# Cross-covariance attention on one core: Q and K of four units loaded in rows of 8 KB, in another order of all work

## The chip, the cores and the metric

The kernel runs on one core of a Trainium2 chip. The metric is the device time of one execution in microseconds (us), as a median of runs; lower is better. Engines are named as in the profile: PE (TensorE), DVE (VectorE), ACT (ScalarE), POOL (GpSimd), SP (SyncE, which here only issues transfers).

## The reference

Batch 8, heads 12, sequence 512, head size 64, all in float32. Attention runs over the channels of a head, not over its rows:

```python
Q_norm = Q / (np.linalg.norm(Q, axis=-2, keepdims=True) + 1e-10)
K_norm = K / (np.linalg.norm(K, axis=-2, keepdims=True) + 1e-10)
attn = np.einsum('bhnd,bhne->bhde', Q_norm, K_norm)
attn = np.exp(attn - np.max(attn, axis=-1, keepdims=True))
attn = attn / (np.sum(attn, axis=-1, keepdims=True) + 1e-10)
return np.einsum('bhnd,bhde->bhne', V, attn).astype(np.float32)
```

Q, K, V and the output have 12.6 MB each, so 37.7 MB are read and 12.6 MB written.

## The kernel before

**Units.** The 96 heads are cut into S = 12 units of eight heads, and two units make a pair `w` (W = 6). One load brings 1 MB: Q of a unit, K of a unit, or half of a pair's V. On 128 partitions a unit of Q has four heads with 32 partitions each and 16 rows of the sequence in each partition, twice (`r` = 0, 1), once for either four heads; so a partition gets two runs of 16 x 64 floats, 4 KB each (`Qf`, `Kf`). V (`Vu`) lies with 16 partitions to a head and 32 rows in each, one run of 8 KB. Unit 0 comes in halves (`FINE`), and its loads are issued ahead of everything else, K's by ACT.

**Steps of a unit `s`.**
- `cast_qk` (keys `q0` for Q, `ck` for K): float32 to bf16, by DVE, ACT or POOL.
- `square` (`sq`, `sk`): squares of the bf16 tiles, by ACT or DVE. `sums` (`s1`) adds them over the rows on PE with the mask `hm`; `fold` (`rd`, DVE), `norms` (`nn`, PE) and `powers` (`pw`, ACT: logarithm and exponent) turn the sums into reciprocal norms.
- `grams` (`gr`): 64 matmuls, K transposed times Q, for two heads at a time (128 x 128, of which the two diagonal 64 x 64 blocks count).
- `scale_k` (`kx`, DVE), `logits` (`lg`: four transpositions on PE), `scales_q` (`qs`, two on DVE), `exps` (`ex`, ACT), `normalise` (`nm`, DVE) give the attention matrix `ab` in bf16.
- V of a pair: `cast_v` (`cv`), `vtrans` (`vt`, transposition on PE), `vcopy` (`vc`).
- `outs` (`ou`, PE) and `ocopy` (`oc`, ACT or DVE) make the output tile `so`, and `store` (`st`) writes it: 1 MB for a unit, in halves for units 10 and 11 (`HALF`), in four cuts for unit 9 (`SPLIT`, `CUTS`).

**Buffers.** Seven tiles of 1 MB for Q and K (`qk`), three for V (`v`), two each of the bf16 tiles of Q and K (`qm`) and of the squares (`sq`), six for output (`so`). `gram` holds four banks of PSUM, one tile in all.

**What sets the order.** The schedule is written out before the program is built. `piece` gives each step a key, a cost on each engine that may do it, the steps that it waits for (`after`), those that it only follows (`behind`), and a rank. `Order.run` plays the schedule with these costs: it takes the steps that could begin soonest, within 0.05 us, and of them the one of lowest rank; `BIAS` moves a choice between engines. The result fixes the order of instructions on every engine, SP's issues among them. Ranks come from `R`; those of loads and stores come from paces: a load of Q or K of unit `s` has `QK_PACE * s / 12`, one of V has `V_FROM + V_PACE * w / 6` (half a pair counts one half), a store `V_FROM + V_PACE * (s / 2) / 6 + ST_LAG`. SP works its list in order: a load that waits for a buffer keeps all later issues back. At most eight transfers are under way.

Of the kernel before, what the change touches and what calls it, by code (L numbers as in the profile page):

```python
# [18 lines left out]
 'R': {'ck': 14.3601,  # L19
       'q': -46.9145,  # L20
       'sq': -4.5261,
       'sk': 21.309,
       'gr': 31.9137,
       's1': -8.269,
       'rd': 14.1273,
       'nn': -13.565,
       'pw': -22.1669,
       'kx': 16.8281,
       'lg': -36.3133,
       'qs': 14.727,  # L30
       'ex': 7.4539,
       'nm': 23.5766,
       'cv': -5.1919,
       'vt': 13.5707,
       'vc': 31.4911,
       'ou': -17.6156,
       'oc': 6.4318},
 'BIAS': {('cv', 'DVE'): 12.3272,
          ('vc', 'ACT'): 5.2627,
          ('oc', 'DVE'): 7.9654,  # L40
          ('q0', 'ACT'): -9.0842,
          ('sk', 'ACT'): 4.174,
          ('sk', 'DVE'): 5.4091,
          ('cv', 'ACT'): 0.906,
          ('cv', 'POOL'): -0.1651,
          ('ck', 'DVE'): -11.8527,
          ('ck', 'ACT'): -10.4645,
          ('ck', 'POOL'): -15.4937,
          ('oc', 'ACT'): 4.7795,
          ('sq', 'DVE'): -12.3114,  # L50
          ('sq', 'ACT'): -21.9953,
          ('q0', 'DVE'): -28.6804,
          ('q0', 'POOL'): -29.3142,
          ('vc', 'DVE'): -20.4676},
 'QK_PACE': 0.9356,
 'V_FROM': 0.0874,
 'V_PACE': 0.7666,
 'ST_LAG': 6.0835,
 'SPLIT': 3,
 'HALF': (10, 11),  # L60
 'WAKE': ('SP',),
 'CUTS': ((0, 0, 6, 0, 124), (0, 0, 6, 124, 128), (0, 6, 16, 0, 128), (1, 0, 16, 0, 128))}
# [89 lines left out]
def kernel(  # L152
# [27 lines left out]
    qmp = ctx.enter_context(tc.tile_pool(name="qmp", bufs=NB["qm"]))  # L180
    sqp = ctx.enter_context(tc.tile_pool(name="sqp", bufs=NB["sq"]))
    vtp = ctx.enter_context(tc.tile_pool(name="vtp", bufs=NB["vt"]))
    sop = ctx.enter_context(tc.tile_pool(name="sop", bufs=NB["so"]))
    abp = ctx.enter_context(tc.tile_pool(name="abp", bufs=NB["ab"]))
# [28 lines left out]
    def load_qk(s, x, c):  # L213
        w, e = divmod(s, 2)
        if (s, x) not in qk32:
            qk32[s, x] = qp.tile([128, T, D], F32, name="qk32")
        issue = nc.scalar if (s, x) == (0, 1) and PAR["ACTQ"] else nc.sync
        o = qk32[s, x][:, cols(c)].rearrange("p t d -> p (t d)")
        i = (Qf, Kf)[x][w, e]
        if c is None:  # L220
            issue.dma_start(out=o.rearrange("p (r x) -> p r x", r=2), in_=i)
        else:
            issue.dma_start(out=o, in_=i[:, c])
# [20 lines left out]
    def cast_qk(eng, s, x, c):  # L244
        if (s, x) not in qkb:
            qkb[s, x] = qmp.tile([128, TT, 2, D], BF16, name="qb" if x == 0 else "kb")
        copy(eng, qkb[s, x][:, :, heads(c)], qk32[s, x][:, cols(c)].rearrange("p (r t) d -> p t r d", t=TT))

    def square(eng, s, x, c):
        if s not in sq:  # L250
            sq[s] = sqp.tile([128, 2, TT, 2, D], BF16, name="sq")
        o, i = sq[s][:, x, :, heads(c)], qkb[s, x][:, :, heads(c)]
# [12 lines left out]
    def sums(s):  # L265
        st[s] = ps_l.tile([D, 4, 2 * D], F32, name="l")
        for t in range(0, TT, 4):
            for x in range(2):
                nc.tensor.matmul(st[s][32 * x:32 * (x + 1)].rearrange("p t d -> p (t d)"), hm,  # L269
                                 sq[s][:, x, t:t + 4].rearrange("p t r d -> p (t r d)"), start=(t == 0), stop=(t == TT - 4))  # L270

    def fold(s):
        s2[s] = small.tile([D, 2 * D], F32, name="s2")
        nc.vector.tensor_reduce(out=s2[s], in_=st[s].rearrange("p t d -> p d t"), axis=mybir.AxisListType.X, op=ALU.add)  # L274

    def norms(s):
        nn[s] = ps_l.tile([128, 2 * HU], F32, name="l")
        nc.tensor.matmul(nn[s], s2[s], sel, start=True, stop=True)  # L278

    def powers(s):  # L280
        ln = small.tile([128, 2 * HU], F32, name="ln")
        r12[s] = small.tile([128, 2 * HU], F32, name="r12")
# [3 lines left out]
    def scale_k(s):  # L286
        kqs[s] = small.tile([128, HU, 2 * D], F32, name="kqs")
        nc.vector.tensor_tensor(out=kqs[s], in0=gram[s][:, :, 0], in1=r12[s][:, HU:, None].to_broadcast([128, HU, 2 * D]), op=ALU.mult)  # L288

    def logits(s):  # L290
        for h in range(HU):
            nc.tensor.transpose(gram[s][:, h, 1], kqs[s][:, h], ident)  # L292

    def scales_q(s, r):
# [3 lines left out]
        nc.vector.tensor_tensor(out=ls[s][half], in0=gram[s][half, :, 1, half], in1=r12[s][half, :HU, None].to_broadcast([D, HU, D]), op=ALU.mult)  # L298
# [5 lines left out]
    def normalise(s):  # L304
# [4 lines left out]
        rb = small.tile([128, HU, 2], F32, name="rb")  # L309
        nc.vector.tensor_tensor(out=rb, in0=ri[:, :, None].to_broadcast([128, HU, 2]),  # L310
                                in1=side[:, None, :].to_broadcast([128, HU, 2]), op=ALU.mult)
        ab[s] = abp.tile([128, HU, 2, D], BF16, name="ab")
        nc.vector.tensor_tensor(out=ab[s], in0=ex[s][:, :, None, :].to_broadcast([128, HU, 2, D]),  # L313
                                in1=rb[:, :, :, None].to_broadcast([128, HU, 2, D]), op=ALU.mult)
# [50 lines left out]
    hm = const.tile([128, 32], BF16, name="hm")  # L365
    nc.gpsimd.memset(hm, 0.0)
    own = const.tile([128, HU], F32, name="own")
    nc.vector.tensor_reduce(out=own, in_=ident.rearrange("p (h i) -> p h i", h=HU), axis=mybir.AxisListType.X, op=ALU.add)
    nc.vector.tensor_copy(hm[:, 0:HU], own)
    sel = const.tile([D, 2 * HU], F32, name="sel")  # L370
    for x in range(2):
        nc.gpsimd.tensor_copy(sel[:, HU * x:HU * (x + 1)], ident[0:D, 32 * x:32 * x + HU])
# [6 lines left out]
    def size(key):  # L379
        n = {"gr": 128, "s1": 16, "nn": 4, "lg": 8, "vt": 8, "ou": 32}[key[0]]  # L380
        return n // 2 if key[0] == "vt" and key[-1] is not None else n

    LOCK = {"ck", "q0", "sq", "sk", "nm", "cv"}
# [11 lines left out]
    CHOICE = ("ck", "q0", "sq", "sk", "cv", "vc", "oc")  # L395
# [17 lines left out]
    def uses(i):  # L413
        s, x = divmod(i, 2)
        return every("ck" if x else "q0", s)

    last = None
    for s in range(S):
        for c in parts(s):
            for x in range(2):  # L420
                key = ("l" + "qk"[x], s, c)
                piece(key, {"DMA": 2 * X if c is None else X}, uses(2 * s + x - NB["qk"]), [last],
                      PAR["QK_PACE"] * ((s + 0.5 * (c or 0)) / S), load_qk, s, x, c)
                last = key
    SM = NB["sm"]
    for s in range(S):
        for c in parts(s):
            dve, act, tt = two(c, 0.16, 0.52), two(c, 0.18, 0.84), two(c, 0.16, 0.52)
            for x, (load, cast, sqr, rank) in enumerate((("lq", "q0", "sq", "q"), ("lk", "ck", "sk", "ck"))):
                free = [("gr", s - NB["qm"])] + every(sqr, s - NB["qm"]) if s >= NB["qm"] else []  # L430
                piece((cast, s, c), {"DVE": dve, "ACT": act, "POOL": 2 * dve}, [(load, s, c)] + free, [], R[rank] + 0.01 * s, cast_qk, s, x, c)
                piece((sqr, s, c), {"DVE": tt, "ACT": act}, [(cast, s, c), back("s1", s, NB["sq"])], [], R[sqr] + 0.01 * s, square, s, x, c)
        piece(("gr", s), {"PE": 1.2}, every("ck", s) + every("q0", s) + [back("qs", s, 1, 0), back("qs", s, 1, 1)], [], R["gr"] + 0.01 * s, grams, s)
        piece(("s1", s), {"PE": 1.2}, every("sk", s) + every("sq", s) + [back("pw", s, 1)], [], R["s1"] + 0.01 * s, sums, s)
        piece(("rd", s), {"DVE": 0.69}, [("s1", s), back("nn", s, SM)], [], R["rd"] + 0.01 * s, fold, s)
        piece(("nn", s), {"PE": 0.3}, [("rd", s)], [], R["nn"] + 0.01 * s, norms, s)
        piece(("pw", s), {"ACT": 0.52}, [("nn", s), back("qs", s, SM, 0), back("qs", s, SM, 1)], [], R["pw"] + 0.01 * s, powers, s)
        piece(("kx", s), {"DVE": 0.69}, [("gr", s), ("pw", s), back("lg", s, SM)], [], R["kx"] + 0.01 * s, scale_k, s)
        piece(("lg", s), {"PE": 0.7}, [("kx", s)], [], R["lg"] + 0.01 * s, logits, s)
        for r in range(2):  # L440
            piece(("qs", s, r), {"DVE": 0.43}, [("lg", s), back("ex", s, SM)], [("qs", s, 0)] if r else [], R["qs"] + 0.01 * s, scales_q, s, r)
        piece(("ex", s), {"ACT": 0.425}, [("qs", s, 0), ("qs", s, 1), back("nm", s, SM)], [], R["ex"] + 0.01 * s, exps, s)
        piece(("nm", s), {"DVE": 1.55}, [("ex", s)] + [back("ou", s, NB["ab"], x) for x in range(4)], [], R["nm"] + 0.01 * s, normalise, s)
# [5 lines left out]
    for w in range(W):  # L449
# [9 lines left out]
        for n, (q, f) in enumerate(turns(w)):  # L459
# [3 lines left out]
            else:  # L463
                wait = [("qs", S - 1, 0), ("qs", S - 1, 1)] + ([("vc", w, *turns(w)[n - 4])] if n >= 4 and turns(w)[n - 4][1] is not None else [])
# [57 lines left out]
```

## Time and profile before

| | us |
|---|---|
| median of 3 runs | 127.5 (127.34, 127.5, 127.55) |
| the profiled execution, its own time | 127.3 |
| its span, first to last instruction | 125.2 |
| busy: PE / PEld / DVE / ACT / POOL | 79.2 / 52.6 / 78.9 / 84.9 / 47.5 |
| DMA: bytes, mean rate over the span | 50.59 MB, 404 GB/s |
| DMA packets | 11,785, of which 1,536 of 8 KB |
| granted TensorE clock, mean | 0.875 |

The span leaves out 2.1 us around the first and last instruction. Busy shares are averages over the span; where several engines wait for one another, it is the waits and the queue of transfers that tell which sets the end. Line numbers (L207, L221) are those of the kernel above.

### The profile page before, as it was taken

To read this page: it belongs to the slowest core of one execution; us is meant where nothing else is said; L and a number is where in the kernel's file an instruction comes from. 1 tells how busy PE (TensorE), PEld (TensorE's weight loads), DVE (VectorE), ACT (ScalarE), POOL (GpSimd) and SP (SyncE) were. 2 spreads that over 40 slices of the span, in tenths; PEclk is the share of its full clock that TensorE was granted. 3 is DMA by queue.
4 is the path that set the end of the run, shared out by engine and by line. 5 is a ranking of instruction groups with operands and counts; after the bars stand their busy time and mean duration, and the time that the engine had idled before them with its cause. 6 is when DMAs were issued, how large, how long until landed. Compare 5 with 4: busy or idle time off the path is not lost.

```text
span 125.2 us, 4066 instructions
## 1 busy us (share of the span) xinstructions
PE 79.2 (63%) x1800; PEld 52.6 (42%) x1800; DVE 78.9 (63%) x140; ACT 84.9 (68%) x116; POOL 47.5 (38%) x40
## 2 busy tenths in 40 slices
PE   0019369873598787859637798882898879941000
PEld 0024254561474475538525455461275456630000
DVE  2043475876852989987987599993799978700000
ACT  4068594784698853998799997938958697863000
POOL 3330665382627088061806925065144810000000
PEclk9999955999657999995999999999599999997555
DMA  3999999999999999999999999999999999999993
GB/s 129 399 419 431 424 411 418 427 419 415 420 424 423 420 428 408 421 414 428 410 432 424 410 421 415 429 414 420 427 428 410 416 416 414 418 408 412 415 395 154
DMA packets 11785, 50.59 MB, mean 404 GB/s; under 512 B 888, under 2 KB 1016, under 8 KB 10232
## 3 DMA queue, kind: packets, MB, share of 16 engines
q1 hardware_dynamic: 11480, 49.29, 95.8%
q10 hardware_dynamic: 288, 1.05, 2.3%
q8 instruction: 14, 0.23, 0.7%
q14 instruction: 3, 0.02, 0.0%
HBM read 37.75 MB, written 12.58 MB: 402 GB/s over the span
## 4 chain that ended last, share of the span: by engine, by line
DMA 70%; PE 9%; ACT 5%; DVE 4%; issue 2%; SPq 1%; ACTq 0%
DMA qk<-in_Q_dram 37%; DMA out_dram<-so 17%; DMA qk<-in_K_dram 16%; ACT so L207 5%; PE po L341 3%; PE gram L263 2%; PE gram L292 1%; PE vps L326 1%; DVE kqs L288 1%; DVE qb L209 1%; PE l L269 1%; DVE ab L313 1%; DVE s L274 0%; PE l L278 0%; ACT ln L283 0%
## 5 line engine op out<-in xcount | busy, mean ns | idle before, releaser
L211 POOL TENSOR_SCALAR kb<-qk 128x2048 bf16<-128x2048 f32 (+1 forms) x13 | 23.0, 1771 | 37.8 <-DMA qk<-in_K_dram 30.9
L254 ACT ACTIVATE sq<-qb 128x2048 bf16<-128x2048 bf16 (+1 forms) x13 | 23.1, 1776 | 7.8 <-DVE qb L209 7.6
L207 ACT COPY so<-po 128x512 f32<-128x512 f32 x47 | 25.6, 584 | 3.9 <-PE po L341 2.3
L211 POOL TENSOR_SCALAR vb<-v 128x1024 bf16<-128x1024 f32 x15 | 21.4, 1444 | 13.4 <-DMA v<-in_V_dram 9.6
L341 PE MATMUL po<-ab,vt 128*32 128x128 bf16 x768 | 20.2, 232 | 6.6 <-ACT so L207 2.1
L263 PE MATMUL gram<-qb,kb 32*128 32x128 bf16 x768 | 15.5, 237 | 12.3 <-DVE qb L209 8.8
L209 DVE CAST qb<-qk 128x2048 bf16<-128x2048 f32 (+1 forms) x12 | 13.7, 1143 | 11.2 <-DMA qk<-in_Q_dram 10.7
L326 PE MATMUL vps<-ident,vb 128*128 128x128 f32 x96 | 17.3, 305 | 4.7 <-POOL vb L211 2.7
L269 PE MATMUL l<-sq,hm 128*32 128x512 bf16 x96 | 18.4, 442 | 1.7 <-ACT sq L254 1.6
L263 PEld LDWEIGHTS <-kb 32*128 32x128 bf16 x768 | 13.3, 104 | 14.4 <-POOL kb L211 10.3
L341 PEld LDWEIGHTS <-vt 128*32 128x32 bf16 x768 | 13.8, 101 | 12.4 <-issue 7.9
L209 DVE COPY vt<-vps 128x1024 bf16<-128x1024 bf16 (+1 forms) x25 | 16.5, 665 | 3.4 <-PE vps L326 3.1
L207 ACT CAST vb<-v 128x1024 bf16<-128x1024 f32 x9 | 12.1, 1341 | 8.8 <-DMA v<-in_V_dram 8.6
L254 ACT ACTIVATE sq<-kb 128x2048 bf16<-128x2048 bf16 (+1 forms) x10 | 17.3, 1733 | 0.6 <-POOL kb L211 0.6
L326 PEld LDWEIGHTS vps<-ident,vb 128*128 128x128 f32 x96 | 11.2, 151 | 8.5 <-POOL vb L211 3.2
L274 DVE TENSOR_REDUCE s<-l 64x128 f32<-64x512 f32 x12 | 8.1, 677 | 6.5 <-PE l L269 6.5
L298 DVE TENSOR_TENSOR ls<-gram,r 64x256 f32<-64x256 f32 x24 | 10.1, 420 | 2.2 <-PE gram L292 1.9
L292 PE MATMUL gram<-ident,kqs 128*128 128x128 f32 x48 | 9.0, 316 | 3.5 <-DVE kqs L288 3.0
L288 DVE TENSOR_TENSOR kqs<-gram,r 128x512 f32<-128x512 f32 x12 | 8.3, 689 | 3.7 <-ACT r L284 3.1
L313 DVE TENSOR_TENSOR ab<-ex,rb 128x512 bf16<-128x512 f32 x12 | 9.3, 773 | 0.4
L269 PEld LDWEIGHTS <-hm 128*32 128x32 bf16 x96 | 5.5, 104 | 9.4 <-issue 7.4
L292 PEld LDWEIGHTS gram<-ident,kqs 128*128 128x128 f32 x48 | 5.7, 154 | 7.4 <-DVE kqs L288 6.6
(25 smaller groups left out, 40.2 us busy)
## 6 DMA issues: line engine op xcount, KB each, us to landing
v<-in_V_dram SPq DMA_DIRECT2D x12, 1024.0 KB, 19.8
qk<-in_Q_dram SPq DMA_DIRECT2D x11, 1024.0 KB, 19.8
qk<-in_K_dram SPq DMA_DIRECT2D x11, 1024.0 KB, 19.6
out_dram<-so SPq DMA_DIRECT2D x9, 1024.0 KB, 19.7
out_dram<-so SPq DMA_DIRECT2D x5, 512.0 KB, 9.4
qk<-in_K_dram ACTq DMA_DIRECT2D x2, 512.0 KB, 4.6
qk<-in_Q_dram SPq DMA_DIRECT2D x2, 512.0 KB, 6.3
out_dram<-so SPq DMA_DIRECT2D x1, 320.0 KB, 10.1
```

The lines of the kernel that those rows point to most:

```text
L207: nc.scalar.copy(o, i)
L209: nc.vector.tensor_copy(o, i)
L211: nc.gpsimd.tensor_scalar(out=o, in0=i, scalar1=1.0, scalar2=0.0, op0=ALU.mult, op1=ALU.add)
L254: nc.scalar.activation(o, i, AF.Square)
L263: nc.tensor.matmul(gram[s][:, h, 0], k, q, start=(t == 0), stop=(t == TT - 1))
L269: nc.tensor.matmul(st[s][32 * x:32 * (x + 1)].rearrange("p t d -> p (t d)"), hm, sq[s][:, x, t:t + 4].rearrange("p t r d -> p (t r d)"), s ...
L288: nc.vector.tensor_tensor(out=kqs[s], in0=gram[s][:, :, 0], in1=r12[s][:, HU:, None].to_broadcast([128, HU, 2 * D]), op=ALU.mult)
L292: nc.tensor.transpose(gram[s][:, h, 1], kqs[s][:, h], ident)
L298: nc.vector.tensor_tensor(out=ls[s][half], in0=gram[s][half, :, 1, half], in1=r12[s][half, :HU, None].to_broadcast([D, HU, D]), op=ALU.mult)
L313: nc.vector.tensor_tensor(out=ab[s], in0=ex[s][:, :, None, :].to_broadcast([128, HU, 2, D]), in1=rb[:, :, :, None].to_broadcast([128, HU, ...
L326: nc.tensor.transpose(ps[:, n], vb[w][:, j].rearrange("p r d c -> p (r d c)").bitcast(F32), ident)
L341: nc.tensor.matmul(po[s, x][32 * h:32 * (h + 1), j].rearrange("p r d -> p (r d)"), v, ab[s][:, h].rearrange("p r d -> p (r d)"), start=Tru ...
```

## The change

Q and K of the pairs 1 and 2 (units 2 to 5, `LONG`) are laid out as V is: a unit is 128 consecutive rows of 8 KB, 16 partitions to each of eight heads, 32 rows of the sequence in each partition (`Ql`, `Kl`). The other eight units keep their layout.

With 16 partitions to a head, two heads share a group of 32 partitions, so in a `LONG` unit:
- Q is cast twice (`mask_q`, keys `q0` and `q1`), each time multiplied by a mask `par` that keeps one head of each two; its square is taken from the float32 tile, and by ACT alone.
- A gram matmul multiplies K by both masked copies at once: 256 columns in place of 128, the same 64 matmuls.
- `scale_k` takes the diagonal blocks in two operations on 64 partitions each and puts them into one tile `kqs` for the pair; `logits` of both units then run as plain matmuls against `eye2`, which joins the two halves, so they wait for both units of the pair (`place`).

For all units: squares of Q and K get tiles of their own (half as large, still two), `sums` is one step for Q and one for K, with four matmuls each that write four groups of partitions, `fold` and `norms` follow that shape, `kqs` is one tile for a pair with a single buffer, and `normalise` drops `rb` and multiplies twice by `scalar_tensor_tensor` instead. The set-up makes more constants (`hm`, `head`, `par`, `both`, `sel`, `eye2`).

All ranks and biases are other numbers (they were within 47 of zero, now within 238), and so is the order of every engine's work. Stores, the cuts at the end and the loads issued ahead are as they were.

```diff
@@ PAR
- 'R': {'ck': 14.3601,
...
+ 'R': {'ck': -70.6322,
...
- 'QK_PACE': 0.9356,
- 'V_FROM': 0.0874,
- 'V_PACE': 0.7666,
- 'ST_LAG': 6.0835,
+ 'QK_PACE': 29.6629,
+ 'V_FROM': 2.146,
+ 'V_PACE': 15.1271,
+ 'ST_LAG': 32.6489,
  'SPLIT': 3,
+ 'GL': 2.0,
+ 'NM': 1.38,
+ 'LONG': (1, 2),
+ 'XL': 1.245,
...
@@ layout, loads, casts, squares
+    LONG = tuple(2 * w + r for w in PAR["LONG"] for r in range(2))
...
+    Ql, Kl = (x.rearrange("b h (p t) d -> (b h p) (t d)", t=T).rearrange("(s p) x -> s p x", p=128) for x in (Q, K))
...
-        if c is None:
+        if s in LONG:
+            issue.dma_start(out=o, in_=(Ql, Kl)[x][s])
+        elif c is None:
...
+    def mask_q(eng, s, r):
+        if (s, 0) not in qkb:
+            qkb[s, 0] = qmp.tile([128, 2, T, D], BF16, name="qb")
+        o, i, m = qkb[s, 0][:, r], qk32[s, 0], par[:, r:r + 1]
+        if eng == "ACT":
+            nc.scalar.activation(o, i, AF.Copy, scale=m)
+        else:
+            (nc.vector if eng == "DVE" else nc.gpsimd).tensor_scalar(out=o, in0=i, scalar1=m, scalar2=0.0, op0=ALU.mult, op1=ALU.add)
...
+        if s in LONG:
+            o, i = sq[s, x].rearrange("p t r d -> p (t r) d"), qkb[s, 1] if x else qk32[s, 0]
@@ grams, sums
-                q, k = (qkb[s, x][32 * h:32 * (h + 1), t].rearrange("p r d -> p (r d)") for x in range(2))
-                nc.tensor.matmul(gram[s][:, h, 0], k, q, start=(t == 0), stop=(t == TT - 1))
...
+                if s in LONG:
+                    o = gram[s][:, h, 0:2]
+                    q, k = qkb[s, 0][p, :, 2 * t:2 * t + 2].rearrange("p r t d -> p r (t d)"), qkb[s, 1][p, 2 * t:2 * t + 2].rearrange("p t d -> p (t d)")
...
+        for n in range(4):
+            b = 32 * (2 * x + n % 2)
+            nc.tensor.matmul(st[s][b:b + 32], m, sq[s, x][:, 4 * n:4 * n + 4].rearrange("p t r d -> p (t r d)"), start=(n < 2), stop=(n >= 2))
@@ scale_k, logits, normalise
+        if s in LONG:
+            half = (LO, HI)[n]
+            nc.vector.tensor_tensor(
+                out=kqs[w][half].rearrange("p (g x) (r d) -> p r g x d", x=2, r=2)[:, r], in0=gram[s][half, :, 0:2, half],
+                in1=r12[s][half, 2 * HU:].rearrange("p (g x) -> p g x", x=2)[:, :, :, None].to_broadcast([D, HU, 2, D]), op=ALU.mult)
...
+    def place(s):
+        return (s | 1, 2 + s % 2) if s in LONG else (s, 1)
...
+            if s in LONG:
+                nc.tensor.matmul(gram[g][:, h, slot, LO], k, eye2, start=True, stop=True)
+            else:
+                nc.tensor.transpose(gram[g][:, h, slot], k, ident)
...
-        rb = small.tile([128, HU, 2], F32, name="rb")
...
+        for r in range(2):
+            nc.vector.scalar_tensor_tensor(out=ab[s][:, :, r], in0=ex[s], scalar=side[:, r:r + 1], in1=ri[:, :, None].to_broadcast([128, HU, D]),
+                                           op0=ALU.mult, op1=ALU.mult)
@@ the schedule
-        return every("ck" if x else "q0", s)
+        return every("ck", s) if x else every("q0", s) + (every("q1", s) + every("sq", s) if s in LONG else [])
...
+                if long:
+                    piece(("q1", s, c), {"DVE": dve, "ACT": act, "POOL": 1.6 * dve}, [(load, s, c)] + free, [], R[rank] + 0.01 * s, mask_q, s, 1)
...
-        piece(("lg", s), {"PE": 0.7}, [("kx", s)], [], R["lg"] + 0.01 * s, logits, s)
...
+        for i in ((s - 1, s) if lng and s % 2 else () if lng else (s,)):
+            piece(("lg", i), {"PE": 1.4 if lng else 0.7}, sum((kx(j) for j in ((s - 1, s) if lng else (s,))), []), [], R["lg"] + 0.01 * i, logits, i)
...
```

More of the change, by code (lines that the diff above doesn't have):

```diff
@@ L18 @@
  'X': 1.27,
- 'R': {'ck': 14.3601,
[L20 to L54, printed above, removed]
@@ L261, in grams @@
             for h in range(HU):
-                q, k = (qkb[s, x][32 * h:32 * (h + 1), t].rearrange("p r d -> p (r d)") for x in range(2))
-                nc.tensor.matmul(gram[s][:, h, 0], k, q, start=(t == 0), stop=(t == TT - 1))
[L265 to L270, printed above, removed]
+                p = slice(32 * h, 32 * (h + 1))
@@ L439 @@
-        piece(("lg", s), {"PE": 0.7}, [("kx", s)], [], R["lg"] + 0.01 * s, logits, s)
[L440 to L443, printed above, removed]
+                long = s in LONG and x == 0
@@ new lines @@
+        lng = s in LONG
+        if lng and s % 2:
+            before = kx(s - 1)
+        else:
+            before = sum((qs(i) for i in range(s - 2 if s - 1 in LONG else s - 1, s)), [])
+        piece(("gr", s), {"PE": PAR["GL"] if lng else 1.2}, every("ck", s) + every("q0", s) + (every("q1", s) if lng else []) + before, [],
+              R["gr"] + 0.01 * s, grams, s)
+        for x in range(2):
+            piece(("s1", s, x), {"PE": 0.6}, every("sk" if x else "sq", s) + [back("pw", s, 1)], [], R["s1"] + 0.01 * s, sums, s, x)
@@ new lines @@
+        piece(("rd", s), {"DVE": 0.69}, [("s1", s, 0), ("s1", s, 1), back("nn", s, SM)], [], R["rd"] + 0.01 * s, fold, s)
+        piece(("nn", s), {"PE": 0.3}, [("rd", s)], [], R["nn"] + 0.01 * s, norms, s)
+        users = kx(s - SM)
+        for i in (range(2 * ((s - SM) // 2), 2 * ((s - SM) // 2) + 2) if s - SM in LONG else (s - SM,)):
+            users = users + [q for q in qs(i) if s - SM not in LONG or q[2] == (s - SM) % 2]
+        piece(("pw", s), {"ACT": 0.52}, [("nn", s)] + users, [], R["pw"] + 0.01 * s, powers, s)
```

160 lines of the change are left out of this document (122 added, 38 removed).

## Prediction

> **What bounds the kernel now.** I read the page's slices and DMA queues first, then the DMA view of short stretches, the timeline of SP, the chain of waits and the table by stage.
>
> ```profile
> DMA  3999999999999999999999999999999999999993
> GB/s 129 399 419 431 424 411 418 427 419 415 420 424 423 420 428 408 421 414 428 410 432 424 410 421 415 429 414 420 427 428 410 416 416 414 418 408 412 415 395 154
> ...
> q1 hardware_dynamic: 11480, 49.29, 95.8%
> ```
>
> The 16 DMA engines are full from the second slice to the last but one. 50.3 MB must cross, and at some 420 GB/s that alone is 120 us of a span of 125.2. Busy shares of the others (ACT 68%, PE and DVE 63%, POOL 38%) leave room on average. So the kernel can gain only by bytes that move faster or by a shorter start or end; it can lose wherever the queue runs dry.
>
> How fast do rows of 8 KB and of 4 KB move? The DMA view of 12.6 to 15 us (V rows alone), then of 25.2 to 32 us (Q and K rows all but three):
>
> ```profile
> DMA packets 138, 1.02 MB, mean 423 GB/s; under 512 B 14, under 2 KB 14, under 8 KB 14
> ...
> q1 hardware_dynamic: 138, 1.02, 100.1%
> ```
>
> ```profile
> DMA packets 720, 2.84 MB, mean 417 GB/s; under 512 B 33, under 2 KB 33, under 8 KB 716
> ...
> q1 hardware_dynamic: 719, 2.82, 101.4%
> ```
>
> First: 124 packets of 8 KB share 1.001 x 16 x 2.4 us, 310 ns each (median in the packet records 309). Second: 1.014 x 16 x 6.8 us, less three of 8 KB and 33 tiny ones, over 683, 160 ns each (median 159). Two 4 KB packets take 318 ns where one of 8 KB takes 309.
>
> Next the end: SP's issues, the end of the chain, the table by stage (columns: stretch, length, busy time and count of PE, PEld, DVE, ACT and POOL, clock, DMA share, GB/s), and SP's waits.
>
> ```profile
> 69.95 2.23 SPq L221 DMA_DIRECT2D qk<-in_K_dram  x1
> 72.23 2.29 SPq L237 DMA_DIRECT2D out_dram<-so  x1
> 74.61 3.48 SPq L227 DMA_DIRECT2D v<-in_V_dram  x2
> ...
> 110.46 7.35 SPq L235 DMA_DIRECT2D out_dram<-so  x4
> ```
>
> ```profile
> 113.08 0.59 ACT so L207
> ```
>
> ```profile
> 97.00:114.00 17.00, 12.86 (x398) 8.39 (x386) 10.51 (x22) 13.19 (x25) 3.04 (x2) 1.00 1.03 415
> 114.00:121.00 7.00, 0.00 (x0) 0.00 (x0) 0.00 (x0) 0.00 (x0) 0.00 (x0) 0.53 1.03 414
> 121.00:125.20 4.20, 0.00 (x0) 0.00 (x0) 0.00 (x0) 0.00 (x0) 0.00 (x0) 0.50 0.49 201
> ```
>
> ```profile
> SPq L235 <- DMA out_dram<-so: 6.5, 4, 2.1
> ```
>
> Compute ends at 113.67 and stores alone run for 10 us more. The last four waited for earlier stores to land, not for data. Adding up the sizes issued and subtracting the packets that had ended, the queue never held under 4.4 MB from 6.5 to 97 us, which is 10.5 us of work at 0.42 MB/us, and 1.7 MB (4.1 us) at the last issue, 117.47. From 121 on the engines fall idle one by one, the last packet ending at 124.0.
>
> **The change, part by part.**
>
> *Rows of 8 KB.* Eight loads of 1 MB (Q and K of units 2 to 5) change from 256 packets of 4 KB to 128 of 8 KB, so each of 16 engines has 64 pairs of packets turned into 64 long ones. By the median packet the saving is 64 x (2 x 159 - 309) = 0.58 us. By the rates of the two stretches, 1.0486 MB takes 2.515 us at 417 GB/s and 2.479 at 423: 0.036 a load, 0.29 in all. Packets overlap a little (the shares pass 100%), which the first count ignores; the second stretch has a fetch of code in it (0.9% on another queue). A fit over all windows of 1 us from 4 to 112, solved for the time that each size takes from an engine, gives 158.0 and 308.6 ns, 64 x 7.4 = 0.47 us. I take 0.45 and keep 0.29 to 0.58; the fit lies between. It all shows, since the queue is full wherever these loads can stand.
>
> A rule weighed here: the Trainium skill, "DMA: Bandwidth & Descriptors", section "Why small descriptors are slow (HBM only)", puts a fixed cost of about 3 cycles on each packet. At the 850 MHz of its section "Specifications" 64 packets fewer on each engine would be an estimated 0.23 us; the sum would be 127.27. The trace's 9 ns for each pair speaks for more than that.
>
> *Q twice.* Each of these Q tiles is cast twice under a mask (`mask_q`): one more pass of 128x2048, 1.23 us by DVE's cast row to 1.90 by POOL's. Nothing shows DVE multiplying by a column of scalars from f32; at four times DVE's f32 copy out of PSUM (673 ns for 512) it would be 2.7 us. Four extra passes: 5 to 11 us over some 35 us, on engines of which POOL is busy 13.9 of 25 us from 25 to 50, DVE 18.1, ACT 17.6. Hidden.
>
> *Gram, K scaling and transposition.* A gram matmul gets 256 columns for 128; 64 of them now take 1.07 us of PE at best, 1.90 in the chain. Double at most: +1.1 to 1.9 us on four units, 4 to 8 us, where PE is busy 18.5 of 25. `scale_k` becomes two operations of 512 elements on 64 partitions (689 ns now for 128): +2.8 us of DVE in all. The transposition keeps four matmuls for each unit, with 64 columns: 0.66 us or less.
>
> *Normalisation, all units.* `rb` (315 ns) and the wide product (773) become two products of 256 elements; the nearest row is `ls`, 420 each: 1.09 against 0.84, 3 us of DVE back. Squares and sums keep their number. The set-up gains some nine small operations of 0.17 to 0.29 us on DVE and POOL; DVE idles 4.34 us before its first cast at 6.54. All at nothing.
>
> *Waits added.* Unit 2 gets its logits only when unit 3 is scaled, 4 with 5: a unit's three loads take 7.5 us, so their outputs come some 7.5 to 10 us later. Queued behind on PE are `outs` and `vtrans`; what needs them is the first store, at 72.23, against copies of unit 0 from 23.3 on. Hidden by tens of us. The fp32 Q tile is held until ACT has squared it, and a square waits for the sums of the unit before (square tiles are half as large). So a Q buffer is freed perhaps 5 us later, and SP waits in order behind it with all later loads. Now the longest wait of SP is 4.6 us, and 10.5 us lie in the queue behind such a wait. What is late next is V, then stores: nothing shows until the sum of delays passes the 10.5 us.
>
> *Order.* In both kernels every load ranks before every store (highest load 0.86 against lowest store 6.17; now 27.2 against 34.8), so stores still fill what loads leave. V ranks earlier: its last half came after unit 10, now after unit 6. The last load to land is then K of unit 11, not V: V ends at about 97.0 (POOL's last casts of it start at 97.44), K of unit 11 is cast at 90.16. If K takes the 97.0, its chain by the rows is cast 1.90, square 1.90, sums 1.49, fold 0.68, norms 0.38, powers 0.48, scaling 0.69, transposition 0.66, scales 0.86, exponent 0.43, normalisation 1.45, matmuls 0.42, four copies 2.36 and 0.8 for hand-overs, 14.5 us: done at 111.5, inside the 113.67 of now.
>
> The sum: profiled execution 127.3 (span 125.2 and 2.1 around it) less 0.45 is 126.85. The median, 127.5, lies 0.2 above this execution: 127.05.
>
> **Rivals.**
>
> *Stores late at the end (slower).* If stores are put ahead of the last Q and K, because V is gone and the seven Q/K buffers hold SP back, the last chain starts late. The last copy can move by 3.8 us (113.67 to 117.47) before an issue moves, and 2.4 more before engines run dry (idle from 121.0, less the 1.1 us from first issue to first packet): 6.2. So K of unit 11 decides from a landing after 105.4, 8.4 us after 97.0. A store takes 2.55 us; three more ahead of it are hidden, the fourth shows 1.8 us: 128.85. For it: the longer hold on Q, and only one store stood ahead of the last loads before. Against: all loads rank first, and 14.5 us of chain stand against 27 us of stores after 97. Chance 0.17.
>
> *A hole among the loads (slower).* Several holds on Q add up to more than the 10.5 us; each us over it counts in full. A delay of 12 us gives 128.55. Against it: no wait of SP reaches half of the cover. Chance 0.11.
>
> *No change.* The rows save less than 0.25 us, or a ragged end eats it (engines end between 121 and 124, so one slow engine hides what 15 gained): 127.5. If the loads were still cut into 4 KB packets the result would be the same; the V rows of equal form, which are 8 KB packets, speak against that. Chance 0.15.
>
> Its rule stands in the same page of the Trainium skill, section "Specifications": transfers from 512 B on run at line rate, so that 4 KB rows would have nothing to gain. The 423 against 417 GB/s contradict it mildly.
>
> **Numbers.** The forecast, 0.29 to 0.58 us saved with the end unchanged, has 0.57. It gives 127.05; its own range is 126.7 to 127.25, with 0.15 for the scatter of the runs (127.34 to 127.55) at the low end. What a measurement here can tell from no change is about 0.2%, 0.26 us. Faster 0.57, same 0.15, slower 0.17 + 0.11 = 0.28. The range goes from 126.7 to 128.9, over the fourth store and the 12 us hold; some 0.1 lies above and 0.05 below.
>
> **What would show it.** Right: 1024 packets fewer (10,761 for 11,785), the DMA row of nines unbroken, copies of outputs ending before 119.9, the last packet near 123.5. A digit under 9 in the middle of the DMA row, or a store of units 10 and 11 that waits for a copy and not for a landing, would show the rivals. The prediction is wrong if the long rows take over 316 ns each, or if the idle time of the DMA engines from 2 to 121 us grows.

## The result, and the profile after

The changed kernel is slower: median 138.75 us of 6 runs (131.91 to 140.76) against 127.5 of 6 (127.31 to 128.35). The ratio is 1.036, 95% interval 1.033 to 1.039; it compares only the shorter executions (131.91 and 132.2 of the changed kernel), while the profiled one (140.76, span 139.0) is one of the longer, and why they lie up to 9 us apart is open. A second set of runs gave 139.29 (137.94 to 140.77).

The page of the changed kernel: busy time of each engine, the slices of DMA, and the packets.

```profile
PE 90.6 (65%) x1824; PEld 61.8 (44%) x1824; DVE 92.1 (66%) x159; ACT 85.6 (62%) x111; POOL 57.2 (41%) x43
...
DMA  4999999999999999999999999999998007736992
GB/s 177 395 423 417 441 424 422 429 424 427 424 420 434 409 434 409 421 419 429 410 420 423 421 429 408 431 409 417 421 414 338 14 0 298 304 120 207 386 417 94
DMA packets 10762, 50.60 MB, mean 364 GB/s; under 512 B 888, under 2 KB 1016, under 8 KB 8184
```

The packets are as many as forecast, and they move as fast: median 159 ns for 4 KB, 309 for 8 KB. But the row of nines breaks. The engines were full to 104 us, as before; from 107.7 to 114.7 next to nothing moved, and the stores that followed came singly. Of the engines DVE grew most, by 13.2 us, and PE next, by 11.4; that the span grew by a like 13.8 shows no cause yet.

SP's timeline and its waits (engine, line, releaser: us in total, times, the longest) show where the hole is.

```profile
82.09 0.37 SPq L235 DMA_DIRECT2D qk<-in_K_dram  x1
84.16 0.34 SPq L241 DMA_DIRECT2D v<-in_V_dram  x1
84.55 39.14 SPq L251 DMA_DIRECT2D out_dram<-so  x9
```

```profile
SPq L241 <- DVE vb L221: 28.0, 6, 9.2
SPq L251 <- ACT so L219: 19.6, 2, 16.7
```

All loads are issued by 84.5 us. The nine whole stores are spread over 39 us, and one of them waits 16.7 us for a copy: between 97.59 and 114.70 SP issues nothing. Before that, loads of V waited 28 us in all for DVE, which had not yet cast the V in the buffer. The copies that this store waits for are those of unit 6, and they are ACT's. PE had made the first two of their four inputs by 98.66; ACT took them up at 112.02, behind the squares of units 9 to 11, which stand ahead of them in its list. Two lines of ACT, then two of POOL (Q and K of unit 11):

```profile
110.22 1.89 ACT L287 ACTIVATE sq<-kb 128x2048 bf16<-128x2048 bf16 x1
112.02 1.05 ACT L219 COPY so<-po 128x512 f32<-128x512 f32 x2
```

```profile
105.43 2.53 POOL L223 TENSOR_SCALAR qb<-qk 128x2048 bf16<-128x2048 f32 x1 [2.85 <-issue]
107.93 1.90 POOL L223 TENSOR_SCALAR kb<-qk 128x2048 bf16<-128x2048 f32 x1
```

The square of unit 11's K needs the cast that ends at 109.83. POOL began these two casts when PE's grams of unit 9 (104.20 to 105.27) had freed a bf16 tile, and those waited for DVE's `scales_q` of unit 8, which ended at 104.05. The hole lies behind ACT's list, and ACT's list behind DVE's. The copy that the last store needs:

```profile
130.28 0.59 ACT so L219
```

It ends at 130.87, 17.2 us later than before. By stage (columns as in the prediction):

```profile
97.00:114.00 17.00, 13.26 (x318) 8.95 (x308) 15.47 (x28) 14.49 (x18) 8.49 (x4) 0.99 0.62 249
114.00:121.00 7.00, 4.40 (x182) 3.36 (x182) 6.23 (x17) 4.90 (x12) 0.00 (x0) 1.00 0.67 269
```

While the transfers starve (shares of 0.62 and 0.67), DVE is busy 15.47 of 17 us and 6.23 of 7, 90%. ACT has 85% in the first stretch and 70% in the second, and PE's clock is granted in full. What is DVE doing that it did not do? The groups of DVE and POOL by form, after (operation, tiles and shapes, count | busy, mean ns | idle before):

```profile
L376 DVE SCALAR_TENSOR_TENSOR ab<-ex,side,rinv 128x256 bf16<-128x256 f32 x24 | 19.1, 838 | 0.5
L221 DVE CAST vb<-v 128x1024 bf16<-128x1024 f32 x17 | 15.8, 970 | 7.4 <-DMA v<-in_V_dram 7.2
L221 DVE COPY so<-po 128x512 f32<-128x512 f32 x7 | 4.8, 689 | 0.9 <-PE po L404 0.7
...
L223 POOL TENSOR_SCALAR qb<-qk 128x2048 bf16<-128x2048 f32 x7 | 14.7, 2098 | 31.2 <-issue 27.9 <-DMA qk<-in_Q_dram 2.5 <-POOL kb L223 0.7
```

Before, in the same view:

```profile
L209 DVE CAST qb<-qk 128x2048 bf16<-128x2048 f32 x10 | 12.2, 1225 | 6.2 <-DMA qk<-in_Q_dram 5.6 <-PE po L341 0.5
...
L313 DVE TENSOR_TENSOR ab<-ex,rb 128x512 bf16<-128x512 f32 x12 | 9.3, 773 | 0.4
...
L310 DVE TENSOR_TENSOR rb<-rinv,side 128x8 f32<-128x8 f32 x12 | 3.8, 315 | 0.4
```

DVE gained 17 casts of V (+15.8; it had none), six more copies of outputs (+4.1), the second operation of `scale_k` (+2.7), 6.0 in the normalisation (19.1 against 9.3 + 3.8), one masked cast (1.3) and small work (1.0). It lost the plain casts of Q (13.7) and three squares of K (3.7). Nearly all of that exchange comes from numbers in `BIAS`, not from the new layout: V's cast on POOL is biased by 41.3 where it was -0.2, Q's on DVE by 6.5 where it was -28.7. Q's casts went to POOL, which casts K already, and V's left POOL for DVE; `nolong` below, without the layout, has 15 of the 17 there too.

The last term is not one of count. The 24 products have a median of 485 ns, a mean of 838 and a longest of 2,128. Timelines of DVE, then POOL, around the normalisation of unit 1:

```profile
39.70 0.18 DVE L373 RECIPROCAL rinv<-z 128x4 f32<-128x4 f32 x1
39.92 3.56 DVE L376 SCALAR_TENSOR_TENSOR ab<-ex,side,rinv 128x256 bf16<-128x256 f32 x2
43.40 0.68 DVE L221 COPY vt<-vps 128x1024 bf16<-128x1024 bf16 x1
```

```profile
36.77 4.41 POOL L277 TENSOR_SCALAR qb<-qk,par 128x2048 bf16<-128x2048 f32 x2 [3.33 <-PE gram L302]
41.15 2.06 POOL L223 TENSOR_SCALAR kb<-qk 128x2048 bf16<-128x2048 f32 x1
```

The two products need 0.97 us alone. They took 3.56. POOL's masked pass ended at 41.18 and its next, the cast of K, at 43.21; the records of the single instructions put the ends of the two products at 41.45 and 43.48, each 0.27 us behind one pass. Below, *hold* is the sum over all instructions of an engine of what each took above the shortest of its form (same operation, tiles and shapes): 3.9 us on DVE before, 13.7 after, of which 8.6 in these products and 3.8 in casts of V. So 9.8 us of what DVE gained is hold. Without holds the durations of its instructions add up to 78.2 us before and 84.0 after. (Records of neighbours overlap a little, so busy times are some us below such sums.)

### The profile page after: what moved, and what is told of

Its sections match the earlier page's. It is cut to its first block, busy times and chain, and to the rows that moved or that the text cites. A ratio compares the mean times of both kernels' runs of the same rounds, so it can differ in the third digit from the quotient of the medians.

```text
span 139.0 us, 4151 instructions
## 1 busy us (share of the span) xinstructions
PE 90.6 (65%) x1824; PEld 61.8 (44%) x1824; DVE 92.1 (66%) x159; ACT 85.6 (62%) x111; POOL 57.2 (41%) x43
## 5 line engine op out<-in xcount | busy, mean ns | idle before, releaser
L223 POOL TENSOR_SCALAR qb<-qk 128x2048 bf16<-128x2048 f32 (+1 forms) x9 | 16.8, 1864 | 34.2 <-issue 27.9
L404 PEld LDWEIGHTS <-vt 128*32 128x32 bf16 x768 | 15.2, 112 | 22.6 <-issue 13.6
L302 PE MATMUL gram<-qb,kb 32*128 32x128 bf16 (+1 forms) x768 | 21.4, 275 | 5.2 <-DVE ls L362 5.1
L287 ACT ACTIVATE sq<-kb 128x2048 bf16<-128x2048 bf16 (+1 forms) x13 | 23.0, 1770 | 0.0
L302 PEld LDWEIGHTS <-kb 32*128 32x128 bf16 x768 | 17.3, 112 | 11.1 <-issue 9.3
L277 POOL TENSOR_SCALAR qb<-qk,par 128x2048 bf16<-128x2048 f32 x7 | 15.8, 2264 | 15.7 <-PE gram L302 10.1
L287 ACT ACTIVATE sq<-qb 128x2048 bf16<-128x2048 bf16 (+1 forms) x9 | 15.5, 1720 | 9.2 <-POOL qb L223 6.5
L221 DVE CAST vb<-v 128x1024 bf16<-128x1024 f32 x17 | 15.8, 970 | 7.4 <-DMA v<-in_V_dram 7.2
L376 DVE SCALAR_TENSOR_TENSOR ab<-ex,side,rinv 128x256 bf16<-128x256 f32 x24 | 19.1, 838 | 0.5
L315 DVE TENSOR_REDUCE s<-l 128x128 f32<-128x512 f32 (+1 forms) x12 | 8.2, 686 | 5.4 <-PE l L310 5.1
L367 ACT ACTIVATE ex<-ls 128x256 f32<-128x256 f32 x12 | 5.0, 416 | 5.8 <-DVE ls L362 4.5
## 6 DMA issues: line engine op xcount, KB each, us to landing
qk<-in_K_dram SPq DMA_DIRECT2D x11, 1024.0 KB, 15.8
```

The lines of the kernel that those rows point to most:

```text
L221: nc.vector.tensor_copy(o, i)
L223: nc.gpsimd.tensor_scalar(out=o, in0=i, scalar1=1.0, scalar2=0.0, op0=ALU.mult, op1=ALU.add)
L277: (nc.vector if eng == "DVE" else nc.gpsimd).tensor_scalar(out=o, in0=i, scalar1=m, scalar2=0.0, op0=ALU.mult, op1=ALU.add)
L302: nc.tensor.matmul(o, k, q, start=(t == 0), stop=(t == TT - 1))
L315: nc.vector.tensor_reduce(out=s2[s], in_=st[s].rearrange("p (t d) -> p d t", d=d), axis=mybir.AxisListType.X, op=ALU.add)
L376: nc.vector.scalar_tensor_tensor(out=ab[s][:, :, r], in0=ex[s], scalar=side[:, r:r + 1], in1=ri[:, :, None].to_broadcast([128, HU, D]), op ...
```

## The experiments

The expectations speak of theories by letters. P: the order, in which POOL's passes come back to back and hold DVE. L: the long layout and its waits for a pair. C: PE and its clock. S: the sum of DVE's work, holds included, on an engine that works its list in order. H: the holds alone. Each kernel ran beside the kernel before on the same chip. DVE sums, holds and last copies are those of the profiled execution, whose time is given too; the ratio stands where the runs give one.

| kernel | median us (range) | ratio (95%) | profiled us | DVE busy, hold | last copy ends |
|---|---|---|---|---|---|
| before | 127.5 (127.31 to 128.35) |  | 127.3 | 78.9, 3.9 | 113.7 |
| the change | 138.75 (131.91 to 140.76) | 1.036 (1.033 to 1.039) | 140.76 | 92.1, 13.7 | 130.9 |
| `rows4` | 127.03 (126.93 to 127.71) | 0.9974 (0.9961 to 0.9986) | 127.71 | 79.1, 4.0 | 114.5 |
| `rows11` | 126.60 (126.41 to 126.64) | 0.9929 (0.9913 to 0.9945) | 126.64 | 78.7, 3.8 | 112.8 |
| `nolong` | 136.04 (134.88 to 137.98) | 1.064 (1.060 to 1.069) | 135.57 | 87.0, 13.0 | 125.4 |
| `qdve` | 137.85 (133.62 to 140.0) |  | 133.62 | 95.2, 7.4 | 123.0 |
| `pooldose` | 132.57 (128.01 to 135.42) | 1.0085 (1.0044 to 1.0126) | 134.52 | 91.4, 16.9 | 124.0 |
| `halfgram` | 140.91 (137.0 to 143.51) |  | 137.0 | 91.5, 12.7 | 126.5 |
| `tt` | 137.45 (132.44 to 138.26) |  | 138.16 | 91.6, 14.0 | 128.2 |
| `nmact` | 155.17 (153.52 to 156.32) | 1.208 (1.204 to 1.212) | 156.32 | 71.5, 3.1 | 147.6 |
| `after2` | 139.29 (137.94 to 140.77) | 1.082 (1.078 to 1.087) | 137.94 | 92.2, 14.0 | 128.1 |
| `dvedose` | 142.56 (142.21 to 145.06) | 1.118 (1.115 to 1.121) | 145.06 | 105.4, 15.3 | 136.3 |
| `cvoff` | 135.06 (129.16 to 137.4) |  | 129.16 | 74.4, 7.1 | 118.8 |
| `long12` | 129.61 (128.98 to 132.69) | 1.014 (1.011 to 1.018) | 132.41 | 78.1, 7.5 | 123.3 |
| `long123` | 128.68 (126.88 to 132.74) | 0.997 (0.994 to 1.001) | 127.11 | 76.5, 5.8 | 118.2 |
| `long1` | 126.97 (126.86 to 127.09) | 0.9961 (0.9936 to 0.9987) | 126.97 | 75.1, 12.1 | 116.3 |

### Long rows alone: `rows4`, `rows11`

The kernel before, with units 2 to 5 (`rows4`) or 1 to 11 (`rows11`) loaded in rows of 8 KB, and nothing else changed.

```diff
...
-        if c is None:
+        if s in (2, 3, 4, 5):
+            issue.dma_start(out=o, in_=(Ql, Kl)[x][s])
+        elif c is None:
```

> The kernel before in its own order, with only the eight loads of Q and K of units 2 to 5 in rows of 8 KB; the rows then land in another arrangement than the casts and sums assume, so the values of these units are not the reference's, and no instruction changes. Theory A (the packets of 8 KB save what the prediction's first term says): 0.29 to 0.58 us less than before, 126.9 to 127.2. Rival (the ragged end of the DMA engines or the rate hides it): within 0.2 us of 127.5.

> The same with all 22 loads of units 1 to 11. Theory A: 22 x (0.036 to 0.072) = 0.8 to 1.6 us less than before, 125.9 to 126.7. Rival (no gain from longer rows, or a limit other than the packets): within 0.3 us of 127.5.

Measured: 0.33 us less for eight loads (0.0026 x 127.4) and 0.9 less for 22, that is 0.041 us a load both times. The page of `rows11`:

```profile
DMA packets 8969, 50.59 MB, mean 406 GB/s; under 512 B 888, under 2 KB 1016, under 8 KB 4600
```

The first term of the sum stands, near the low end of its 0.29 to 0.58. So the whole loss comes from the rest.

### The order without the layout: `nolong`

All of the changed kernel, its ranks and biases too, with no unit in long rows; the schedule is written anew by the same rules.

```diff
- 'LONG': (1, 2),
+ 'LONG': (),
```

> The changed kernel with no unit in long rows (LONG empty): all its ranks, biases, smaller square tiles, single scaling buffer and new normalisation, the order planned again from these. Theory P (the order is what costs: POOL takes the casts of Q as well as K, and DVE's normalisation stands still while POOL works): still late, 129 to 134 us, with normalisations of over 3 us in the trace. Rival L (the long layout costs: masked passes on POOL, joined pairs): back to 127.3 to 127.8.

Measured: 136.04 (P had 129 to 134), late without a single long row, masked cast or wait for a pair. L is not needed for the loss; whether the layout adds to it in this order stays open, since the scatter covers the 2.7 us between the medians.

### The casts of Q back on DVE: `qdve`

```diff
+            if key[0] == "q0" and key[1] not in LONG and eng == "POOL":
+                eng = "DVE"
```

> The changed kernel in its own written order, with the Q casts of the eight other units moved from POOL to DVE at the place that they have in the order. Theory P: POOL no longer works for 4 us on end in these units, the normalisations that took 4.2 us (of units 3 and 5) come back to 1.6 to 2.2, and the time falls by 3 us or more below the changed kernel's 131.9 (fast runs), in spite of 11 us more work on DVE. Rival L: no gain or slower, since DVE has more to do: 131.5 to 136.

Measured: 137.85, 133.62 in the profiled execution. The holds fell from 13.7 to 7.4 as P wants, but the fall of 3 us or more below 131.9 did not come. DVE's row in the page says why:

```profile
PE 83.8 (64%) x1824; PEld 57.9 (44%) x1824; DVE 95.2 (72%) x168; ACT 86.2 (66%) x111; POOL 42.4 (32%) x34
```

The casts came back onto an engine that had kept V's. Its sum rose to 95.2. That speaks against holds as the one cause, and for the sum.

### Holds put into the kernel before: `pooldose`

Eleven more passes on POOL, each writing a float32 tile of K over itself ahead of the cast.

```diff
+        if x == 1 and c is None:
+            copy("POOL", qk32[s, x], qk32[s, x])
```

> The kernel before in its own order, with one more POOL pass of 128x2048 behind every K cast of units 1 to 11, which writes the float32 tile of K over itself: 11 passes of about 1.9 us, so that POOL works for some 4 us on end, as with the casts of Q and K one behind the other in the changed kernel. Nothing waits for the pass but the buffer. Theory P (DVE's normalisation and casts stand still while POOL works, and the delay adds up along DVE's list): normalisations of over 2.5 us in several units, DVE's work later by 3 us or more at the end, and 128.5 to 135 us. Rival C (the TensorE clock and the chain are what costs; POOL at 55% is harmless): 127.3 to 127.8.

Measured: 128.01 to 135.42, median 132.57. DVE in the profiled execution (134.52, mean clock 0.887, above the 0.875 of before) does the same work in 12.5 us more:

```profile
PE 81.4 (61%) x1800; PEld 55.7 (42%) x1800; DVE 91.4 (69%) x140; ACT 84.7 (64%) x116; POOL 75.5 (57%) x51
...
L209 DVE CAST qb<-qk 128x2048 bf16<-128x2048 f32 x10 | 20.3, 2030 | 1.8 <-DMA qk<-in_Q_dram 1.8
```

The casts of Q that took 1,225 ns take 2,030, `rb` 499 for 315, the squares 1,847 for 1,226. All six executions are longer than each of the nine of the kernel before beside them (127.28 to 127.62). So passes of POOL that bring nothing to the result can by themselves make this kernel late, with the order of before; by how much varied from 0.7 to 8.1 us, and the ratio of 1.0085 is small.

### Less work for PE: `halfgram`

The changed kernel with every second gram matmul left out.

```diff
-        for t in range(TT):
+        for t in range(0, TT, 2):
...
```

> The changed kernel in its own written order, with every second gram matmul left out: half of the rows of Q and K do not enter the logits. PE has some 11 us less to do and may keep its clock. Rival C (PE, at half clock for part of the time, is what makes the chain late): 127 to 129 us. Theory P: later stages still collide with POOL and the normalisations of over 3 us stay, 130 to 138 us.

Measured: 140.91, although PE fell from 90.6 to 83.7 us (its mean clock was 0.815). PE's work is not what sets the end, so C falls as far as it rests on that. No run sets the clock apart from the rest; the changed kernel's executions had means from 0.812 to 0.869. DVE and POOL again, in `halfgram`:

```profile
70.77 4.12 DVE L376 SCALAR_TENSOR_TENSOR ab<-ex,side,rinv 128x256 bf16<-128x256 f32 x2
```

```profile
70.69 1.90 POOL L223 TENSOR_SCALAR qb<-qk 128x2048 bf16<-128x2048 f32 x1 [7.48 <-PE gram L302]
72.55 2.06 POOL L223 TENSOR_SCALAR kb<-qk 128x2048 bf16<-128x2048 f32 x1
```

POOL began 0.08 us ahead of the product. POOL's passes ended at 72.59 and 74.62, the products at 72.86 and 74.89: again 0.27 us behind, one pass for each product.

### The form of the normalisation: `tt`, `nmact`

`tt` is the changed kernel with the old `rb` and one wide product; `nmact` has ACT do the products (a scaling of `ri` and eight of 128x64, for each `r`).

```diff
-            nc.vector.scalar_tensor_tensor(out=ab[s][:, :, r], in0=ex[s], ...)
...
+            nc.scalar.activation(rb, ri, AF.Copy, scale=side[:, r:r + 1])
+            for h in range(HU):
+                nc.scalar.activation(ab[s][:, h, r], ex[s][:, h], AF.Copy, scale=rb[:, h:h + 1])
```

> The changed kernel in its own written order, with the two last operations of the normalisation as before the change (rb, then one product of 512). Theory P: DVE has one long product in place of two shorter ones that POOL can come between, so one stall less for each normalisation: 129 to 132 us in fast runs. Rival C: no difference to the changed kernel, 131.9 (fast runs).

> The changed kernel in its own written order, with the two products of each normalisation made by ACT in ten short operations, in place of DVE's two. Theory P: no DVE operation of the normalisation can be held by POOL any more; the 8.6 us of excess in them is gone and the time falls to 127 to 130 us, unless the 20 us more on ACT become the new chain. Rival C: the changed kernel's 131.9 (fast runs) or more, since ACT has more to do.

Measured: 137.45 for `tt` (P had 129 to 132), with the holds moved to `ab` (5.1) and `rb` (4.1). The form is not the cause. `nmact` took DVE's sum to 71.5 and its holds to 3.1, and was the slowest of all:

```profile
PE 95.7 (62%) x1824; PEld 65.4 (42%) x1824; DVE 71.5 (46%) x135; ACT 115.1 (75%) x231; POOL 55.8 (36%) x43
```

ACT, with 29.5 us more, took DVE's place. The test missed its aim, since it moved the load to another engine without room.

### The changed kernel again: `after2`

> The changed kernel once more, beside the next three on one chip, for a trace of one of its faster executions. All theories: 131 to 141 us. Theory P expects that in a faster execution fewer normalisations and casts of DVE are held by POOL, and that the sum of what they are held for, with the slack at the end, accounts for the difference.

Measured: 139.29, with DVE at 92.2, hold 14.0, last copy 128.1: the picture of the first set.

### DVE's work alone: `dvedose`

The order of before, each copy of V out of PSUM made twice by DVE. The copy reads PSUM, adds no work to POOL and moves nothing to another engine.

```diff
+        copy(eng, o.rearrange("p j x c -> p (j x c)"), vps[w, q, f].rearrange("p j x -> p (j x)").bitcast(BF16))
```

> The kernel before in its own order, with each copy of a transposed V out of PSUM made twice by DVE: 25 copies, 16.5 us more for DVE, none of a kind that was seen held by POOL. Theory S (what counts is DVE's work and holds together, about 79 us on time and from 87 on late): DVE at some 95 us, the last output copy at 121 to 126 us and 129 to 136 us. Theory H (only the holds by POOL make DVE late): 127.3 to 128, with the copies hidden.

Measured: 142.56, all four between 142.21 and 145.06. The page:

```profile
PE 87.0 (61%) x1800; PEld 59.6 (42%) x1800; DVE 105.4 (74%) x165; ACT 85.3 (60%) x116; POOL 51.0 (36%) x40
...
DMA  5999999999999999999999999999991005457893
```

DVE's sum rose by 26.5 us, 16.7 of it in the copies. The last copy moved by 22.6, the time by 15, and the DMA row shows the same hole: for an engine at 63% busy, more work was far from free. S had the direction, but it had DVE at some 95 us and 129 to 136 us. The rest came from holds, which rose from 3.9 to 15.3 us although POOL got no more work: 4.6 in casts of Q, 3.6 in `rb`, 3.1 in the wide products, 2.5 in squares. So the dose put in work and holds together and can't tell S from H. That it was the later places of DVE's steps that brought them beside POOL's passes is likely and was not tried.

### Casts of V taken off DVE: `cvoff`

The changed order, V's casts on DVE given to ACT (9) and POOL (8).

```diff
+            if key[0] == "cv" and eng == "DVE":
+                eng = ("ACT", "POOL")[key[3]]
```

> The changed kernel in its own written order, with the 17 V casts of DVE given to ACT (9, the first half of a tile) and POOL (8, the second half). Theory S: DVE falls to about 80 us, and the time to 127 to 130. Theory H: POOL works 11 us more and holds the normalisations as often or more often, so 131 to 140 as now. A third outcome, ACT or POOL as the new bound, would show in their busy times (ACT over 100).

Measured: 129.16 in the profiled execution, 133.97 to 137.4 in the other three; S had 127 to 130, H 131 to 140. The page of the one that was profiled:

```profile
PE 77.1 (61%) x1824; PEld 53.0 (42%) x1824; DVE 74.4 (58%) x142; ACT 95.6 (75%) x120; POOL 64.9 (51%) x51
...
DMA  4999999999999999999999999999999999987992
```

Its fastest is 2.75 us below the fastest of the changed kernel, its median 3.7 below. With DVE at 74.4 the last copy came at 118.8, and the hole is nearly closed. But ACT now has 95.6 us, and why the other executions took 5 to 8 us more no profile here shows. So moving the casts off gives back part, and whether the engine that took them sets the rest is open.

### The layout in other orders: `long12`, `long123`, `long1`

The changed kernel with other ranks, biases and paces, with no cast of V on DVE: the same four units in long rows, six units, or only units 2 and 3.

```diff
...
- 'LONG': (1, 2),
+ 'LONG': (1,),
...
- 'BIAS': {('cv', 'DVE'): 2.9846, ('cv', 'POOL'): 41.3259, ...
+ 'BIAS': {('cv', 'DVE'): 16.0349, ('cv', 'POOL'): 2.0164, ...
```

> The changed kernel, the same four units in long rows, with other ranks and biases: Q and K casts stay on POOL, but DVE casts no V (ACT 15, POOL 9) and three of the four second masked passes, so it has few operations that POOL can hold. Theory P (the order of work and where DVE meets POOL cost the time, not the layout): 126.9 to 127.6, the DMA row unbroken. Rival L (pairs joined, masked passes and wider grams cost by themselves): 129 us or more. In between: it is faster than the changed kernel and still late by one or two stalls, 128 to 130.

> Six units in long rows (pairs 1 to 3), again with other ranks and biases, no V cast on DVE (POOL 15, ACT 9) and the second masked pass on DVE. Theory P: 126.6 to 127.6; by the run of rows alone the four more loads are worth another 0.16 us. Rival L: later than with four units, 130 us or more.

> Two units in long rows (pair 1), other ranks and biases, no V cast on DVE (POOL 18, ACT 6). Theory P: 127.1 to 127.6, half of the gain of four units. Rival L: between the kernel before and four units in long rows, 128 us or more.

Measured: 129.61, 128.68 and 126.97. The page of `long1`:

```profile
PE 78.1 (62%) x1812; PEld 53.4 (43%) x1812; DVE 75.1 (60%) x134; ACT 86.5 (69%) x117; POOL 72.1 (58%) x58
...
DMA  3999999999999999999999999999999999999993
```

It is 0.4% faster than before. It has holds of 12.1 us and POOL does 15 us more than in the changed kernel; but DVE's sum, holds included, is 75.1, and the row of nines is whole. `nolong` has holds of 13.0 and is 8.6 us late. H can't tell these two apart; S can, for `nolong` has 87.0. `long123`, with six units, has executions down to 126.88, so the layout does not make a kernel late by itself. `long12` is a miss for P and S, and L had its 129 or more: with DVE at 78.1 in a profiled execution of 132.41 its last copy came at 123.3. ACT had 94.2 us there, but in `cvoff`, with 95.6, the last copy came at 118.8; the cause is open.

The fastest kernel of all is `rows11` at 126.60; it has no part of the change but the rows.

## Why the prediction was wrong

**The rows: right.** Forecast 0.45 us (0.29 to 0.58), measured 0.33 in `rows4`, with the packets as forecast. The fit and the packet medians were high, the rates of the two stretches (0.29) nearer.

**"The others leave room on average": wrong, and the root of it.** The prediction read shares of the span: DVE 63%, so hidden. But DVE works one list in order, and what comes late on it keeps loads of V waiting (28 us of SP) and then, through PE, POOL and ACT, the stores. The margin is that of the prediction's own first rival: the last copy may move by 6.2 us before the end does. In the profiles, all kernels with a DVE sum under 80 had their last copy at 118.8 or earlier, but for `nmact`, where ACT had 115.1, and `long12`; from 87 up all had it at 123.0 or later. Nothing was measured between, and this is a pattern over kernels that differ in more than DVE's sum.

**The part on *Order*: the step that failed.** It costed the new ranks and biases by two checks, whether loads rank before stores and how long the last chain is. It did not ask which engine each cast now goes to, though the biases stand in the diff, and it had no term for what DVE stands still when its steps meet POOL's. V's casts off POOL and Q's onto it put 15.8 us on DVE and took 13.7 away, beside +2.7 of `scale_k` and +4.1 of copies. The prediction counted the `scale_k` term (2.8) and called it hidden. The holds, +9.8, are the larger part of what DVE gained.

Adding up the work alone would not have shown it. By the costs in the kernel's own planner DVE has 80.2 us before and 81.2 after, and its play ends the last copy at 115.1 and 116.5; the planner even keeps POOL's passes and DVE's casts, squares and normalisations apart (`port`, `LOCK`). On the chip the last copies end at 113.7 and 130.9. The kernel before is never more than 2.5 us behind its plan on DVE. The changed one is 16.6 behind when unit 7's `fold` starts at 90.9, and stays 15 to 17 behind to the end. The normalisations of units 1, 3 and 5 make 6.8 of the 16.6 by lasting longer than planned; most of the rest is waiting. `long1`, whose plan gives DVE 66.0, falls 5.0 behind, with much the same holds, and is level again at its last step. So the loss was made in the first 91 us, on a list without room to make it up.

The last chain, 14.5 us by the rows, took 23 from K's cast to the last copy (107.93 to 130.87). And that cast itself was the larger delay: K of unit 11 was issued at 82.09 and landed 8.6 us later. Nor was it the last load to land, as forecast: V's last half was issued behind it, at 84.16.

**The normalisation: sign wrong.** "3 us of DVE back" took 1.09 us before, an average with 0.23 of hold in it for each unit (166 and 691 ns are the shortest of the two), and 0.84 after, from a row (`ls`) that reads PSUM. Alone the two products take 0.97, and in place they took 1.59: +6.0 us. The sign of a hold was in the trace of before, unread:

```profile
17.99 1.19 DVE L310 TENSOR_TENSOR rb<-rinv,side 128x8 f32<-128x8 f32 x1
```

An operation of 166 ns took 1.19 us, to 19.18, beside a pass of POOL from 17.89 to 19.23. The Trainium skill, "SBUF — State Buffer", section "Who interferes with whom", has the rule: a DVE instruction with two inputs in SBUF shares ports with GpSimd's reads, whoever issues first keeps them for the whole instruction, and the other stands still. The runs agree, with 485 ns alone against up to 2,128 behind a pass of POOL. By itself the rule would not have given the loss, since `long1` has holds of 12.1 us to the changed kernel's 13.7 and is on time.

**Q twice: the price too high, the conclusion too light.** The masked cast takes DVE 1.29 us (one), not 2.7, and POOL 2.26 (seven). The four extra passes, three of them on POOL, were called hidden because the engines had room. POOL had; DVE, whose products stood still behind POOL's passes, did not. `nolong` is late without them, so they are not needed for the loss.

**Waits and cover.** SP's 10.5 us of queue did cover the loads: the row of nines holds to 104 us. It was spent by then, and stores waited for outputs.

**The rivals.** "Stores late at the end" named the place: a last copy after 119.9 and a store of the last units that waits for a copy. Its mechanism (K of unit 11 landing late behind stores) did not occur, K being in SBUF 17 us before its cast, and its 128.85 priced one store, not a late engine. No rival had an engine's work and holds in it, and the range ended 10 us short.

## What to carry to other kernels

When a change redraws a schedule, read from the biases or ranks which engine each step goes to, and add up each engine's whole list, before and after; an in-order engine at 63% busy can be full, and its margin is how far its last result may move before the end does, not its idle share. Work alone can come out even, as here; add what the engine will stand still for. For that, look for instructions of one form whose durations differ, and see which engine's pass ends with them. Where a plan exists, compare it with the trace step by step: where the lag begins is where the time goes, and the hole in the transfers can come much later. A dose of harmless work in the kernel before (`dvedose`, `pooldose`) shows how much room a list has, if what else grew is read too; moving work to another engine (`nmact`, `cvoff`) tests that engine as well.

## What the runs showed of the hardware

While DVE waits for POOL and POOL has a next pass ready, POOL's pass went ahead of DVE's next instruction in these traces: two products that need 0.97 us together took 3.56 and 4.12 us, one POOL pass for each product. Smallness is no protection: `rb`, 8 elements a partition, took 166 or 1,191 ns. POOL's masked pass was not steady either: 1.97 us at the shortest and 3.05 at the longest.
